# A 352-byte filler taken out of the constants, and two sets of small tiles moved into them: large left-side tiles from offset 32 (and 224, 160) to offset 0 of a 256-byte step

## The chip, the cores and the metric

The kernel runs on one core of one Trainium2 chip. Times are device microseconds (us) of one launch. A core has five engines with queues of their own: PE (TensorE, matrix products), ACT (ScalarE), DVE (VectorE), POOL (GpSimd) and SP (SyncE, which here issues every DMA). PE's product takes two operands from SBUF: one is loaded beforehand as weights (the profile has these loads as a row of their own, PEld), the other streams through (the moving operand). Results land in PSUM.

SBUF has 128 partitions; a tile takes the same bytes in each of them. "Offset" below always means a tile's first byte within the partition, and mostly what is left of it after division by 256.

## The reference, cut to what matters

One transformer block, batch 1, 1024 tokens, width 1024, all in float32:

```
mod = silu(c) @ w_ada + b_ada                       # six vectors: shift, scale, gate, twice
h   = rmsnorm(x, g) * (1 + sc1) + sh1
proj = h @ w_in                                     # attention q k v, delta q k v z, two gates
y_attn  = dilated attention, 8 heads, three branches merged by their log-sums
y_delta = gated delta rule, 8 heads, chunks of 64   # a recurrence over the chunks
x = x + g1 * (concat(y_attn, y_delta) @ w_out)
h = rmsnorm(x, g_ffn) * (1 + sc2) + sh2
x = x + g2 * ((silu(h @ w_gate) * (h @ w_up)) @ w_down)
out = rmsnorm(x, final_g)
```

## The kernel before

**Precision.** Every large product is made of three products in the faster float32r format: each operand is split into a high part (a rounded copy, made by ACT) and a low part (the rest, a subtraction on DVE or POOL), and high x high, high x low and low x high are added up in PSUM. So a weight block arrives by DMA in a raw tile `wr`, becomes `wh` and `wl`, and is used.

**Order of the work.** First the projections with the modulation (to about 135 us of the span). Then the delta rule's chunks, into whose gaps PE's projections for attention are filled by a table of due times (to 460 us); attention with the same filling (to 690 us); the output projection (to 749 us). Then the FFN. Its up products are arranged as a Strassen-like scheme with blocks called H11, H21, H22 and sums T1 to T4: for each of `NF` = 11 column blocks `f`, and for the gate and the up weights, there are seven blocks of 12 matmuls (`up_mm`, lines 1615 to 1625: four k, three products each): H11 and H21 in `up_first`, then T2, T1, T3, H22, T4 in `up_rest`. `up_mm` takes the weights (`wh`, `wl`) as PE's weights and the activations (`bh`, `bl`, halves of the H and T blocks) as the moving operand. The three first column blocks have their H11 and H21 parts done early (`AHEADF`, line 1756); the very first of these (f = 0, gate) has its weights in tiles of their own, `eh` and `el` (`slab_early`, line 1540). From 1172 us on come the down products (`down_mm`, line 1818, seven runs X, Y, X, Y2 (named Z in the profile), X, Z, X, with a tail W whose operands were prepared early, line 1839), and the last norm.

**How tiles are placed.** Pools on the left side of SBUF are stacked from the bottom, those on the right side from the top. The constants' pool `cp` is the lowest on the left; everything else on the left stands on it, so the size of the constants shifts all of it. By the program's list of placed tiles each tile's bytes are rounded up to 32. Offsets of the large tiles in the program before:

| pool, side | holds | first byte modulo 256 |
|---|---|---|
| `cp`, left | constants: `ident` and `onesr` (128), `S`, `beta` and others after the filler (32), `cc` (32) | mixed |
| `pr`, `pd`, left | inputs, delta rule | 32 |
| `pa` up to `sc`, left | attention: `va`, `KL`, `ng`, `X`; of `QS` and `KS` two buffers of three | 32 |
| `pa` after `sc`, left | `et`, `xo`, the third buffer of `QS` and `KS` | 224 |
| `pf`, `po`, `pe`, `px`, `po2`, left | FFN: H11 and H21, `eh`, `el`, sums, raw weights `wr2` | 32 |
| `pz` up to `rn`, left | down stage: gains, sums, `y` | 32 |
| `pz` after `rn`, left | `xr`, `sq3`, the early `wh` and `wl` of the tail W | 160 |
| `hh`, `hl`, `yh`, `yl`, `wp`, `wq`, `pt`, right | activations of the projections, all other `wr`, `wh`, `wl`, and H22, T1 to T4 | 0 |

The pool of the left side's FFN starts at byte 9504 = 37 x 256 + 32. On the right a filler of 224 bytes (line 98) is the first tile; it is not touched.

**Names that the change and the prediction touch.** `const([P, 88], "end")` (line 125) is the filler: 88 x 4 = 352 bytes. `sc` (line 1322, in `att_score`) holds, for one head and one block of 128 queries, the running minimum, the sum and its reciprocal; six buffers of 16 bytes rounded to 32, 192 bytes. `rn` (line 1864) holds the sums of squares of the last norm, 128 bytes.

Of the kernel before, what the change touches and what calls it, by code (L numbers as in the profile page):

```python
# [10 lines left out]
F32 = mybir.dt.float32  # L11
# [7 lines left out]
P = 128  # L19
# [63 lines left out]
def build(tc, I, out):  # L83
# [4 lines left out]
    def pool(name, side="left", bufs=1, space=None):  # L88
        st = ExitStack()
        kw = {} if space is None else {"space": space}  # L90
        p = st.enter_context(
            tc.tile_pool(name=name, bufs=bufs, side=side, reuse_waits="tile", **kw)
        )
        return p, st
# [4 lines left out]
    cp = op(tc.tile_pool(name="cp", bufs=1))  # L99
    dr = op(tc.tile_pool(name="dr", bufs=1, space=DRAM))  # L100

    def const(shape, name, dt=F32):
        return cp.tile(shape, dt, name=name, tag=name)
# [18 lines left out]
    mhalf = const([P, 4], "mhalf")  # L122
    nc.vector.memset(mhalf, -0.5)

    const([P, 88], "end")

    def small(name, shape, src):
        t = const(shape, name)
# [446 lines left out]
    @contextmanager  # L575
    def turn(name):

        with tc.issue_after(last[0].ins) if ahead(FILL.get(name, 0)) else ExitStack():
            yield
# [680 lines left out]
    pa, sa = pool("pa")  # L1260
    turns = [0]

    def scores(name):
        turns[0] += 1
        return abank(name) if turns[0] % 3 == 0 else sbank(name)
# [49 lines left out]
    def att_score(hp, qb, e):  # L1315

        h = 2 * hp + e
        nk = (qb + 1) * P
        qs = slice(qb * P, qb * P + P)
        QS, KS, KL, ng = loaded[hp][1][e]  # L1320
        X = pa.tile([P, T], F32, name=f"X{h}_{qb}", tag="X", bufs=XB)
        sc = pa.tile([P, 4], F32, name=f"sc{h}_{qb}", tag="sc", bufs=6)
        m = None
        for c0 in range(0, nk, HALF):
            c1 = min(nk, c0 + HALF)
            ps = scores(f"S{h}_{qb}_{c0}")
            with turn(f"S{h}_{qb}_{c0}"):
                nc.tensor.matmul(ps[:, 0 : c1 - c0], QS[:, qs], KS[:, c0:c1], start=True, stop=False)
                nc.tensor.matmul(ps[:, 0 : c1 - c0], QS[:, qs], KL[:, c0:c1], start=False, stop=True)  # L1329
            i = c0 // HALF  # L1330
            u = P * (7 - qb)
            nc.vector.tensor_tensor_reduce(  # L1332
                out=X[:, c0:c1], in0=ps[:, 0 : c1 - c0], in1=ng[:, u + c0 : u + c1], scale=1.0,
                scalar=(3e38 if m is None else m), op0=ALU.add, op1=ALU.min, accum_out=sc[:, i : i + 1],
            )
            m = sc[:, i : i + 1]
        nc.scalar.activation(X[:, 0:nk], X[:, 0:nk], AF.Exp, scale=-1.0, bias=m, accum_out=sc[:, 2:3])  # L1337
        nc.vector.reciprocal(sc[:, 3:4], sc[:, 2:3])  # L1338
        nc.gpsimd.tensor_scalar(  # L1339
            out=X[:, 0:nk], in0=X[:, 0:nk], scalar1=sc[:, 3:4], scalar2=0.0, op0=ALU.mult, op1=ALU.add  # L1340
        )
        return X
# [46 lines left out]
    def attend(switch):  # L1389
        units = [(hp, qb) for hp in range(4) for qb in range(TB)]  # L1390
        xs, ets = {}, {}
        for i in range(len(units) + AV):
            if i >= AV and units[i - AV] == (EARLY, 3):
                switch()
            if i < len(units):
                hp, qb = units[i]
                if hp not in loaded:
                    until(lambda: hp in done)
                    loaded[hp] = att_load(hp)
                if i < EARLY * TB + 3 + AV:  # L1400
                    ahead((FRONT - used[0]) / (EARLY * TB + 3 + AV - i))
                if qb >= 2 and hp < 3 and hp + 1 in done and hp + 1 not in loaded:
                    loaded[hp + 1] = att_load(hp + 1)
                xs[i] = [att_score(hp, qb, e) for e in range(2)]
            if AT <= i < len(units) + AT:
                hp, qb = units[i - AT]
                ets[i - AT] = [att_turn(hp, qb, e, xs[i - AT][e]) for e in range(2)]
                del xs[i - AT]
            if i >= AV and units[i - AV][1] % 2:
                hp, qb = units[i - AV]  # L1410
                att_value(hp, qb, [ets.pop(i - AV - 1), ets.pop(i - AV)])
# [385 lines left out]
    pz, sz = pool("pz")  # L1797
# [58 lines left out]
    def sums(name):  # L1856
        return [pz.tile([P, HALF], F32, name=f"{name}_{b}", tag=f"{name}{b}") for b in range(4)]
# [3 lines left out]

    p1, u2, r5 = sums("p1"), sums("u2"), sums("r5")
    y = {(l, s): sums(f"y{l}{s}") for l in range(2) for s in range(2)}
    rn = pz.tile([P, 8, 4], F32, name="rn", tag="rn")

    def x_in(l, s, b):
        x = pz.tile([P, HALF], F32, name=f"xr{l}{s}{b}", tag="xr", bufs=4)
# [160 lines left out]
```

## Time and profile before

| what | value |
|---|---|
| three runs | 1401.86, 1402.77 and 1393.12 us; median 1401.86 |
| the profiled execution's span, first to last instruction | 1389.5 us |
| the profiled execution's own time | about 1402.9 us: its trace's time axis begins 11.0 us before the first instruction, and its clock records end 2.3 us after the last one |
| instructions | 24383 |
| PE busy | 97% of the span, 8984 matmul records |
| DVE, ACT, POOL busy | 63%, 48%, 19% |
| DMA | 244.08 MB by SP's queue, 54.4% of 16 engines' span |
| granted clock of PE | 1.0 except in three stretches at 0.5: 10.2 us from 135.8 us of the span, 3.4 us from 794.5 us, and the last 6.8 us |

How to read it: a busy PE is not PE at its peak, since a matmul's record lasts longer than the time until the next one starts. In the chain of work that ended last, a row such as "PE wua L1622 x12" gives the time from the start of the first of 12 matmuls to the start of what follows, so it divides by 12 into the time from start to start. In a name like `wua<-H11h,wh_wu` the first name is what is written, the second the moving operand, the third the weights. Rows that group by line give minimum, median and maximum of the durations in ns.

### The profile page before, as it was taken

The page shows a single profiled execution, that of the slowest core. Times are in us where ns is not written, and L with a number is a line of the kernel's source. Part 1 is how long each engine was busy: PE and PEld are TensorE (multiplying, and loading weights), DVE is VectorE, ACT ScalarE, POOL GpSimd, SP SyncE. Part 2 cuts the span into 40 slices and gives each one's busy share as a digit, 9 for nine tenths or more (in the row PEclk, how much of TensorE's full clock was granted, in tenths as well). Part 3 has the DMA queues.
Part 4 walks back from the last instruction along what each step waited for, and adds up shares of the span by engine and source line. Part 5 has one row for each costly group of instructions (what it writes and reads, how often), then busy time and mean ns, then how long its engine had stood idle before and what let it go on. Part 6 is the DMA issues. An engine that isn't in the chain of part 4 may idle for free.

```text
span 1389.5 us, 24383 instructions
## 1 busy us (share of the span) xinstructions
PE 1343.3 (97%) x8984; PEld 1106.9 (80%) x8984; DVE 875.5 (63%) x1678; ACT 660.1 (48%) x1285; POOL 266.8 (19%) x250
## 2 busy tenths in 40 slices
PE   8998999999999999899999999999999999999998
PEld 4777887888889877678777788888888888888876
DVE  3687583657846242766258977666675776474497
ACT  4497514347233454775168533333333333444455
POOL 2345303324213433543261000000000000000000
PEclk9999899999999999999999999999999999999999
DMA  8666574476362546522675346444453665765585
GB/s 311 228 194 168 160 213 156 138 235 156 124 165 80 172 134 182 153 91 70 217 230 174 124 143 211 140 156 168 152 174 124 213 209 186 255 222 193 191 270 192
DMA packets 169871, 245.64 MB, mean 177 GB/s; under 512 B 32566, under 2 KB 73831, under 8 KB 169752
## 3 DMA queue, kind: packets, MB, share of 16 engines
q1 hardware_dynamic: 169752, 244.08, 54.4%
q8 instruction: 71, 1.16, 0.3%
q14 instruction: 48, 0.39, 0.1%
HBM read 181.27 MB, written 67.48 MB: 179 GB/s over the span
## 4 chain that ended last, share of the span: by engine, by line
PE 71%; DVE 14%; DMA 5%; ACT 4%; issue 3%; POOL 2%; SPq 0%; POOLq 0%; DVEq 0%; ACTq 0%
PE wua L1622 9%; PE wga L1622 8%; PE X L1822 6%; PE wuc L1622 4%; PE wgc L1622 4%; PE g_a L590 4%; PE wo L590 3%; PE Z L1822 3%; PE y L1373 2%; PE wub L1622 2%; PE wgb L1622 2%; PE Y L1822 2%; DVE tm L899 2%; PE g_va L616 2%; PE f L251 2%
## 5 line engine op out<-in xcount | busy, mean ns | idle before, releaser
L1612 DVE TENSOR_TENSOR wl_db<-wr_db,wh_db 128x512 fp32r<-128x512 f32 x77 | 52.8, 689 | 66.4 <-ACT wh_db L1611 66.4
L1611 ACT CAST wh_db<-wr_db 128x512 fp32r<-128x512 f32 x77 | 47.6, 621 | 86.3 <-PE X L1822 37.8
L1332 DVE CUSTOM_DVE_ANT_0 X<-S,ng 128x512 f32<-128x512 f32 (+3 forms) x64 | 36.6, 587 | 62.7 <-PE S L1329 54.7
L1339 POOL TENSOR_SCALAR X<-X,sc 128x128 f32<-128x128 f32 (+7 forms) x64 | 48.9, 767 | 90.4 <-DVE sc L1338 77.5
L1822 PE MATMUL X<-wl_db,wh_da 128*128 128x512 f32 x160 | 62.4, 390 | 0.3 <-DVE wl_db L1612 0.3
L1337 ACT ACTIVATE X<-X,sc 128x128 f32<-128x128 f32 (+7 forms) x64 | 49.4, 773 | 27.8 <-DVE sc L1332 26.3
L1822 PE MATMUL X<-wh_db,wl_da 128*128 128x512 f32 x160 | 62.3, 389 | 0.0
L1822 PE MATMUL X<-wh_db,wh_da 128*128 128x512 f32 x160 | 62.2, 389 | 0.0
L1612 DVE TENSOR_TENSOR wl_da<-wr_da,wh_da 128x512 fp32r<-128x512 f32 x77 | 52.8, 686 | 4.0 <-ACT wh_da L1611 4.0
L1611 ACT CAST wh_da<-wr_da 128x512 fp32r<-128x512 f32 x77 | 47.5, 617 | 14.2 <-DMA wr_da<-ao_d 7.8
L590 PE MATMUL wo<-yh,wh_wo 128*128 128x512 f32 x128 | 51.9, 406 | 0.0
L590 PE MATMUL g_a<-hh,wh_a 128*128 128x512 f32 x128 | 51.4, 401 | 0.0
L590 PE MATMUL wo<-yh,wl_wo 128*128 128x512 f32 x128 | 51.2, 400 | 0.0
L590 PE MATMUL wo<-yl,wh_wo 128*128 128x512 f32 x128 | 50.5, 395 | 0.5 <-DVE yl L1440 0.5
L590 PE MATMUL g_a<-hl,wh_a 128*128 128x512 f32 x128 | 50.7, 396 | 0.0
L590 PE MATMUL g_a<-hh,wl_a 128*128 128x512 f32 x128 | 50.4, 394 | 0.0
L1352 PE MATMUL tr<-ident,X 128*128 128x128 f32 x288 | 44.1, 277 | 4.7 <-ACT et L1357 2.3
L1611 ACT CAST wh_wg_s<-wg_s 128x512 fp32r<-128x512 f32 x33 | 20.5, 622 | 58.6 <-PE wuc L1622 24.8
L1352 PEld LDWEIGHTS tr<-ident,X 128*128 128x128 f32 x288 | 32.6, 140 | 15.9 <-POOL X L1339 7.2
L1611 ACT CAST wh_wu_s<-wu_s 128x512 fp32r<-128x512 f32 x33 | 20.4, 622 | 45.0 <-PE wga L1622 17.2
L1611 ACT CAST wh_wg<-wr_wg 128x512 fp32r<-128x512 f32 x31 | 19.3, 621 | 46.8 <-PE wua L1622 19.2
L231 POOL TENSOR_TENSOR wl_wo<-wr_wo,wh_wo 128x512 fp32r<-128x512 f32 x24 | 31.9, 1333 | 47.3 <-ACT wh_wo L230 43.1
(554 smaller groups left out, 4345.1 us busy)
## 6 DMA issues: line engine op xcount, KB each, us to landing
wm<-in_wada SPq DMA_DIRECT2D x44, 512.0 KB, 6.7
wr_da<-ao_d SPq DMA_DIRECT2D x77, 256.0 KB, 3.0
wr_wu<-in_wu SPq DMA_DIRECT2D x50, 256.0 KB, 2.8
wr_wg<-in_wg SPq DMA_DIRECT2D x48, 256.0 KB, 3.0
ao_d<-a SPq DMA_DIRECT2D x44, 256.0 KB, 2.5
wr_wd<-in_wdn SPq DMA_DIRECT2D x44, 256.0 KB, 3.0
wr_db<-wt_d SPq DMA_DIRECT2D x44, 256.0 KB, 3.0
ao_d<-as SPq DMA_DIRECT2D x33, 256.0 KB, 2.1
```

Of the source, the lines that this page charges most:

```text
L231: (eng or nc.gpsimd).tensor_tensor(out=lo[:, :n], in0=raw[:, :n], in1=hi[:, :n].bitcast(F32), op=ALU.subtract)
L251: nc.tensor.matmul(first[bank], a[:, w0], b[k][:, cs], start=(k == 0 and n_ == 0), stop=(k == KT - 1 and n_ == 2))
L590: last[0] = nc.tensor.matmul(ps, a[:, w0], b[k0 + k4][:, cs], start=(i == 0), stop=(i == n - 1))
L616: last[0] = nc.tensor.matmul(ps[:, :n], a[k][:, ts_], b[:, w0], start=(i == 0), stop=(i == 23))
L1332: nc.vector.tensor_tensor_reduce(out=X[:, c0:c1], in0=ps[:, 0 : c1 - c0], in1=ng[:, u + c0 : u + c1], scale=1.0, scalar=(3e38 if m is None ...
L1337: nc.scalar.activation(X[:, 0:nk], X[:, 0:nk], AF.Exp, scale=-1.0, bias=m, accum_out=sc[:, 2:3])
L1339: nc.gpsimd.tensor_scalar(out=X[:, 0:nk], in0=X[:, 0:nk], scalar1=sc[:, 3:4], scalar2=0.0, op0=ALU.mult, op1=ALU.add)
L1352: nc.tensor.transpose(ps[:, (kb - c0) * P : (kb - c0 + 1) * P], X[:, kb * P : kb * P + P], ident)
L1611: nc.scalar.copy(hi, src)
L1612: (eng or nc.vector).tensor_tensor(out=lo, in0=src, in1=hi.bitcast(F32), op=ALU.subtract)
L1622: nc.tensor.matmul(ps, a[:, w0], b, start=(first and k == 0 and n_ == 0), stop=(k == 3 and n_ == 2), skip_group_check=True,)
L1822: nc.tensor.matmul(bank[b], a[:, ts_], w, start=(first and n_ == 0), stop=(last and n_ == 2), skip_group_check=True,)
```

## The change

The filler in the constants goes, `sc` is allocated from the constants' pool and no longer from attention's, and `rn` becomes a constant instead of a tile of the last pool. No instruction is added, removed or reordered by the text of the change; only places in SBUF change.

```
@@ -122,7 +122,6 @@
     mhalf = const([P, 4], "mhalf")
     nc.vector.memset(mhalf, -0.5)
 
-    const([P, 88], "end")
 
     def small(name, shape, src):
         t = const(shape, name)
@@ -1319,7 +1318,7 @@
         qs = slice(qb * P, qb * P + P)
         QS, KS, KL, ng = loaded[hp][1][e]
         X = pa.tile([P, T], F32, name=f"X{h}_{qb}", tag="X", bufs=XB)
-        sc = pa.tile([P, 4], F32, name=f"sc{h}_{qb}", tag="sc", bufs=6)
+        sc = cp.tile([P, 4], F32, name=f"sc{h}_{qb}", tag="sc", bufs=6)
         m = None
         for c0 in range(0, nk, HALF):
             c1 = min(nk, c0 + HALF)
@@ -1861,7 +1860,7 @@
 
     p1, u2, r5 = sums("p1"), sums("u2"), sums("r5")
     y = {(l, s): sums(f"y{l}{s}") for l in range(2) for s in range(2)}
-    rn = pz.tile([P, 8, 4], F32, name="rn", tag="rn")
+    rn = const([P, 8, 4], "rn")
 
     def x_in(l, s, b):
         x = pz.tile([P, HALF], F32, name=f"xr{l}{s}{b}", tag="xr", bufs=4)
```

In bytes: the constants lose 352 and gain 192 and 128, together 32 fewer, so what stands on them starts at 9504 - 32 = 9472 = 37 x 256. With `sc` gone from attention's pool, what stood after it moves from 224 to 0, and with `rn` gone from the last pool, what stood after that moves from 160 to 0. The right side stays where it is. Constants between the old filler and the end of the pool move by 352 bytes, from offset 32 to 192 (`S`, for one).

More of the change, by code (lines that the diff above doesn't have):

```diff
@@ L123, in build @@
     nc.vector.memset(mhalf, -0.5)
-    const([P, 88], "end")
     def small(name, shape, src):
@@ L1321, in att_score @@
         X = pa.tile([P, T], F32, name=f"X{h}_{qb}", tag="X", bufs=XB)
-        sc = pa.tile([P, 4], F32, name=f"sc{h}_{qb}", tag="sc", bufs=6)
+        sc = cp.tile([P, 4], F32, name=f"sc{h}_{qb}", tag="sc", bufs=6)
         m = None
@@ L1863, in build @@
     y = {(l, s): sums(f"y{l}{s}") for l in range(2) for s in range(2)}
-    rn = pz.tile([P, 8, 4], F32, name="rn", tag="rn")
+    rn = const([P, 8, 4], "rn")
     def x_in(l, s, b):
```

## The prediction, made before the changed kernel was run

> **What bounds the kernel now.** I read the page first: the span and the chain of work that ended last, by engine and by line.
>
> ```profile
> span 1389.5 us, 24383 instructions
> ...
> PE 71%; DVE 14%; DMA 5%; ACT 4%; issue 3%; POOL 2%; SPq 0%; POOLq 0%; DVEq 0%; ACTq 0%
> PE wua L1622 9%; PE wga L1622 8%; PE X L1822 6%; PE wuc L1622 4%; PE wgc L1622 4%; PE g_a L590 4%; PE wo L590 3%; PE Z L1822 3%; PE y L1373 2%; PE wub L1622 2%; PE wgb L1622 2%; PE Y L1822 2%; DVE tm L899 2%; PE g_va L616 2%; PE f L251 2%
> ```
>
> PE carries 71% of the chain, and the FFN's up blocks (`wua` to `wgb`) are its largest part. The change moves tiles and nothing else, so the question is what an offset costs, and whether PE pays it. Stretches of the span come next; after the borders stand PE, its weight loads, DVE, ACT and POOL (busy, count), then granted clock, DMA share, GB/s.
>
> ```profile
> 135.70:146.00 10.30, 10.30 (x78) 10.30 (x77) 6.76 (x12) 10.30 (x33) 2.88 (x3) 0.50 0.66 154
> 794.50:798.00 3.50, 3.50 (x10) 2.69 (x10) 3.50 (x7) 2.15 (x4) 0.00 (x0) 0.51 0.50 166
> 810.00:1172.00 362.00, 362.00 (x1584) 297.02 (x1583) 245.32 (x383) 132.05 (x226) 0.00 (x0) 1.00 0.50 169
> 1172.00:1375.00 203.00, 201.97 (x885) 165.35 (x885) 134.25 (x226) 103.48 (x194) 0.00 (x0) 1.00 0.68 230
> ```
>
> From 810 to 1172 us, the up products, PE never rests: what a matmul takes there is time of the kernel. DVE is busy 245 of 362 us, so it can feed a PE that is a per cent faster. The two first rows are stretches at half clock; they come back among the rivals.
>
> **The key row.** The chain in order of time shows one pass of the up products, block by block: start, us, what, and how many.
>
> ```profile
> 959.20 2.80 PE wua L1622 x12
> 962.01 2.80 PE wub L1622 x12
> 964.81 2.76 PE wua L1622 x12
> 967.56 2.72 PE wuc L1622 x12
> 970.28 2.72 PE wua L1622 x12
> 973.00 2.72 PE wuc L1622 x12
> 975.72 2.72 PE wua L1622 x12
> ```
>
> All are blocks of 12 matmuls of one shape. In order they are H11, H21, T2, T1, T3, H22, T4. The last four take 2.72 us, 226.7 ns each. H11 and H21 take 2.80 us: 233.4 ns. T2, which follows them, takes 2.76 us. H11 and H21 are the two blocks that stand on the left, at offset 32, with weights from the right, at offset 0; T1 to T4 and H22 stand on the right. That may be the offset, or it may be that these two blocks come first. Durations by operand (minimum/median/maximum, ns):
>
> ```profile
> L1622 PE MATMUL wua<-H11h,wh_wu x44: 393/396/479, 749.3 to 1153.5; 128*128 128x512 f32 x44
> ...
> L1622 PE MATMUL wga<-T4h,wh_wg x44: 389/389/389, 788.2 to 1150.8; 128*128 128x512 f32 x44
> ```
>
> ```profile
> L1822 PE MATMUL W<-wh_db,wh_da x16: 387/389/390, 1371.9 to 1382.1; 128*128 128x512 f32 x16
> ```
>
> W's operands stand on the left too, at offset 160, but both of them: no penalty. So offset from a multiple of 256 isn't the trouble by itself; a difference between the two operands' offsets may be. The pass f = 0 of the gate tests this. There H11 at 32 meets weights `eh` and `el` that are also at 32. PE in order of time, two pairs of rows, each pair seven starts apart:
>
> ```profile
> 741.24 0.39 PE L1622 MATMUL wga<-H11h,el 128*128 128x512 f32 x1
> ...
> 742.83 0.39 PE L1622 MATMUL wgb<-H21h,eh 128*128 128x512 f32 x1
> ```
>
> ```profile
> 940.50 0.40 PE L1622 MATMUL wga<-H11h,wh_wg 128*128 128x512 f32 x1
> ...
> 942.14 0.39 PE L1622 MATMUL wga<-H11l,wh_wg 128*128 128x512 f32 x1
> ```
>
> With `eh` 1.59 / 7 = 227 ns, with `wh_wg` 1.64 / 7 = 234 ns: the same activations from the same place, and only the weights' offset differs. I take it that a matmul of 512 columns in this format takes 6.7 ns more while weights are loaded from another offset, modulo 256, than it streams from.
>
> **The change part by part.**
>
> *H11 and H21 from offset 32 to 0.* Both operands are then at 0. Of 22 passes (11 column blocks, gate and up) one has `eh` and is free of the penalty already: 21 x 2 blocks x (2.80 - 2.72) us = 3.4 us.
>
> *T2 behind them.* Its 2.76 us are, I think, a settling after the slower rhythm: its offsets agree, and it ends at the pace of T1. In the passes f = 3 to 10 it follows H21 directly (f < 3 had H11 and H21 done early): 16 x 0.04 us = 0.6 us. Both terms lie on the path, as PE is busy 362.00 of 362 us there. Together 4.0 us.
>
> *Mixed stages, 135 to 690 us.* Products with operands at 0 alternate with short matmuls on left tiles at 32 or 224. A price falls where one follows the other; by my count in PE's order, with the placements, some 155 matmuls of the fast format have their successor's weights at 32 now. At 6.7 ns that is 1.0 us, at the least nothing; a few scores of `KL` (32) with `QS` at 224 lie inside that. I take 0.5 us. The weights' path into transposes stays unequal (`ident` at 128).
>
> *Constants that lose agreement.* `S` goes to 192 while `kd` and `qd` go to 0; today both are at 32. These are 112 matmuls of 128 columns in plain float32. What unequal offsets cost in that format is seen in transposes against `ident`, at 128 against 32:
>
> ```profile
> L1352 PE MATMUL tr<-ident,X x288: 270/272/332, 466.6 to 651.3; 128*128 128x128 f32 x144
> ```
>
> ```profile
> L998 PE MATMUL st<-S,kd x56: 270/275/348, 253.4 to 445.1; 128*128 128x128 f32 x56
> ```
>
> Unequal 272 ns, equal 275: no price. Taken as 0; at most 112 x 6.7 ns = 0.8 us.
>
> *`sc` and `rn`.* The same instructions, buffers and engines, no new wait. A loss would need slower small operations, and those work on one column wherever they stand.
>
> ```profile
> L1338 DVE RECIPROCAL sc<-sc x64: 142/164/168, 459.9 to 648.7; 128x1 f32<-128x1 f32 x64
> ```
>
> Without `sc` and `rn` below them, attention's later tiles and the last pool's overlap no more of the older tiles than before (I went through the placements); so no transfer waits for more. Taken as 0 on both sides.
>
> *Vector engines.* Subtractions whose source is mostly a raw tile on the right at 0 (first row, some are on the left) and one on the left at 32 (second) take the same:
>
> ```profile
> L1612 DVE TENSOR_TENSOR wl_wu<-wr_wu,wh_wu x33: 679/684/693, 743.9 to 1157.9; 128x512 fp32r<-128x512 f32 x33
> L1612 DVE TENSOR_TENSOR wl_wg_s<-wg_s,wh_wg_s x33: 681/685/695, 767.1 to 1135.7; 128x512 fp32r<-128x512 f32 x33
> ```
>
> Nothing there, and DVE isn't the bound.
>
> *DMAs.* All of 256 KB; columns are KB each and median us to landing.
>
> ```profile
> wr_da<-ao_d SPq DMA_DIRECT2D x77, 256.0 KB, 3.0
> ...
> wr_wd<-in_wdn SPq DMA_DIRECT2D x44, 256.0 KB, 3.0
> ...
> wr_db<-in_wdn SPq DMA_DIRECT2D x33, 256.0 KB, 3.4
> ...
> wr_wo<-in_wo SPq DMA_DIRECT2D x24, 256.0 KB, 2.6
> ...
> xo<-in_xT SPq DMA_DIRECT2D x16, 256.0 KB, 3.4
> ```
>
> `wr_wd` lands on the left at 32, `wr_da` and `wr_db` on the right at 0: the left is no slower, and from the same tensor (`in_wdn`) it is faster. `xo` (left, 224) against `wr_wo` (right, 0) is the one pair that speaks for a price, 0.8 us of 3.4, but its source is read in half rows. DMA has 5% of the chain, 69.5 us; at 0.8 / 3.4 that would be 16 us at most. Two pairs of three show none, so I take 0. [...]
>
> **The sum.** 4.0 + 0.5 = 4.5 us. The profiled execution's own time is about 1402.9 us (span 1389.5, and 13.3 around it), close to the median, so the median can stand for it: 1401.9 - 4.5 = **1397.4 us**, 0.3% less. A measurement of this kernel can tell about 1% from no change.
>
> **The rivals.**
>
> *Nothing changes: 1401.9 us.* The 6.7 ns could belong to the blocks' place in the order, or the tiles could end up elsewhere than the byte sums say. For it: H11 and H21 always come first. Against: the pass with `eh` comes first too and runs at 227 ns. [...] Chance 0.15.
>
> *The clock: 1390.6 us.* The stretches at half clock (10.3 us at 0.50 and 3.5 us at 0.51) cost half their length, 5.1 + 1.7 us. Slightly other timing may do without them: 1397.4 - 6.8 = 1390.6. For it: the fastest of three runs is 8.7 us below the median. Against: two of three runs are not. Chance 0.15.
>
> *DMAs gain as well: 1389.2 us.* If `xo` against `wr_wo` is the true price and half of the chain's DMA time has it, 16 / 2 = 8.2 us go besides. Against: the other pairs, and that PE never rests in the up stage, so nothing there waits for a transfer. Chance 0.10.
>
> *Equal offsets collide: slower, 1413.9 us.* Today DVE and ACT work on the left at 32 while PE reads at 0 on the right; after the change all are at 0. If PE then meets them as it meets its own weight loads now, the 1584 + 885 matmuls from 810 to 1375 us pay 6.7 ns each: 16.5 us. It decides once more than 4.5 us / 6.7 ns = 670 of them pay. Against: T4's 389/389/389 is steady while DVE reads and writes `wr`, `wh` and `wl` at 0. Chance 0.05.
>
> **How the numbers follow.** The forecast has the remaining 0.55; its own range is 1394 to 1400. The range of 1387.5 to 1402.5 takes in the clock case, "nothing" and most of the DMA case; left out are the collision, the far end of the DMA bound, and both rivals with a gain at once. Faster by over 1% means below 1387.8: parts of the clock and DMA cases, 0.09. Slower by over 1% means above 1415.9: 0.02. Within 1%: 0.89.
>
> **What would show it.** In the chain after, H11 and H21 at 2.72 us for 12, T2 at 2.72, the stretch of one pass 0.20 us shorter; `wua<-H11h,wh_wu` at a median of 389. W stays at 389, `st<-S,kd` near 275, DMA landings as they are. Wrong would be: H blocks still at 2.80 (the cause is not the offset), T1 to T4 above 2.72 (collision), or landings on the left shorter by over 0.3 us with a shorter first 135 us (the DMA case).

## The result, and the profile after

| | median of 17 runs | lowest to highest |
|---|---|---|
| before | 1393.4 us | 1388.4 to 1409.3 |
| after | 1385.8 us | 1382.1 to 1394.5 |

The ratio of after to before is 0.9942, with a 95% interval of 0.9923 to 0.9961: 8.1 us gained (5.4 to 10.7), where 4.5 us were forecast. It is inside the 1% of the prediction, but the interval is clear of 1. The three times that the prediction started from had a median of 1401.9 us; 17 have 1393.4. So the kernel came out below the forecast range, at more gain than forecast and from a lower start. Executions more than 1.5% above the fastest of their kernel are left out of every ratio and count below.

The profiled execution after has a span of 1383.3 us, 6.2 less. From the page, with the chain by engine:

```profile
span 1383.3 us, 24383 instructions
...
PE 71%; DVE 14%; DMA 5%; ACT 4%; issue 3%; POOL 2%; SPq 0%; POOLq 0%; DVEq 0%; ACTq 0%
```

The bound is the same. The chain in order of time, the same stretch as in the prediction (line numbers are one lower, since a line is gone):

```profile
955.40 2.72 PE wua L1621 x12
958.12 2.72 PE wub L1621 x12
960.84 2.72 PE wua L1621 x12
963.56 2.72 PE wuc L1621 x12
966.28 2.72 PE wua L1621 x12
969.00 2.72 PE wuc L1621 x12
971.72 2.72 PE wua L1621 x12
```

H11, H21 and T2 took 2.80, 2.80 and 2.76 us and now take 2.72 like the others. The same in two rows of durations:

```profile
L1621 PE MATMUL wua<-H11h,wh_wu x44: 389/389/476, 748.9 to 1147.7; 128*128 128x512 f32 x44
...
L1821 PE MATMUL W<-wh_db,wh_da x16: 389/389/389, 1365.7 to 1375.9; 128*128 128x512 f32 x16
```

H11's median fell from 396 to 389 ns, and W, equal offsets before and after, stayed. How long the up stage is, the first product of the down stage shows (first row before, second after):

```profile
L1822 PE MATMUL X<-wh_db,wh_da x160: 387/389/396, 1170.7 to 1371.2; 128*128 128x512 f32 x160
```

```profile
L1821 PE MATMUL X<-wh_db,wh_da x160: 388/389/389, 1164.7 to 1365.1; 128*128 128x512 f32 x160
```

From the first `wua<-H11h` to the first X it is 1170.7 - 749.3 = 421.4 us before, 1164.7 - 748.9 = 415.8 after: 5.6 less. Windows after, the columns as in the prediction:

```profile
135.70:146.00 10.30, 10.30 (x87) 10.30 (x87) 7.02 (x11) 10.30 (x32) 2.88 (x3) 0.54 0.63 163
794.50:798.00 3.50, 3.50 (x17) 2.88 (x16) 3.50 (x7) 2.32 (x5) 0.00 (x0) 1.00 0.79 241
810.00:1172.00 362.00, 362.00 (x1599) 299.77 (x1598) 246.87 (x386) 133.01 (x228) 0.00 (x0) 1.00 0.51 171
```

The half-clock stretch at 794.5 us is gone (17 matmuls in place of 10, so 7 x 0.227 = 1.6 us); the one at 135.7 is still there. So 5.6 - 1.6 = 4.0 us of the up stage are the blocks, as forecast. In these two executions nothing else is left over: 4.0 + 1.6, 0.4 up to the first `wua`, and 0.2 after the first X make the 6.2. The runs, however, gained 8.1 by the ratio.

Transfers, KB each and median us to landing, after:

```profile
wr_da<-ao_d SPq DMA_DIRECT2D x77, 256.0 KB, 2.9
...
wr_wd<-in_wdn SPq DMA_DIRECT2D x44, 256.0 KB, 3.0
...
wr_db<-in_wdn SPq DMA_DIRECT2D x33, 256.0 KB, 3.4
...
xo<-in_xT SPq DMA_DIRECT2D x16, 256.0 KB, 3.8
```

`xo` went from offset 224 to 0 and lands no sooner (3.4 before). One transfer that the prediction didn't look at does: the second 512 KB into `tn`, where the delta rule's chunk solve begins. Before, then after; the first row is the product that reads it, the second the issue, the third who waited:

```profile
L931 PE MATMUL lv<-tn,dt x64: 191/191/212, 387.0 to 388.0; 32*32 32x32 f32 x64
...
L908 SPq DMA_DIRECT2D tn<-tn_d x1: 370/370/370, 381.3 to 381.3; - x1
...
  PE lv L931: 0.6, 1
```

```profile
L930 PE MATMUL lv<-tn,dt x96: 191/191/212, 386.3 to 395.7; 32*32 32x32 f32 x96
...
L907 SPq DMA_DIRECT2D tn<-tn_d x1: 371/371/371, 381.4 to 381.4; - x1
```

From issue to use that is 5.6 us before and 4.9 after, without rounding, and PE's wait of 0.6 us is gone from the list. The chain that ended last goes through this landing; first before, then after:

```profile
381.35 5.58 DMA tn<-tn_d
```

```profile
381.40 4.78 DMA tn<-tn_d
```

### The profile page after: what moved, and what is told of

It reads as the page before. It is cut to its first block, busy times and chain, and to the rows that moved or that the text cites. A ratio compares the mean times of both kernels' runs of the same rounds, so it can differ in the third digit from the quotient of the medians.

```text
span 1383.3 us, 24383 instructions
## 1 busy us (share of the span) xinstructions
PE 1336.5 (97%) x8984; PEld 1105.9 (80%) x8984; DVE 875.4 (63%) x1678; ACT 659.7 (48%) x1285; POOL 268.4 (19%) x250
## 4 chain that ended last, share of the span: by engine, by line
PE 71%; DVE 14%; DMA 5%; ACT 4%; issue 3%; POOL 2%; SPq 0%; POOLq 0%; DVEq 0%; ACTq 0%
PE wua L1621 9%; PE wga L1621 8%; PE X L1821 6%; PE wgc L1621 4%; PE wuc L1621 4%; PE g_a L589 4%; PE wo L589 3%; PE Z L1821 3%; PE Y L1821 2%; PE wub L1621 2%; PE wgb L1621 2%; PE y L1372 2%; PE g_va L615 2%; DVE tm L898 2%; PE f L250 2%
```

## The experiments

**Theory A** is the prediction's: a matmul of the fast format with 512 columns pays some 6.7 ns while moving operand and weights differ in offset modulo 256. The other theories are in the expectations. "Low" below counts executions with a mean granted clock of 0.990 or less; the expectations' own counts were made on the way, some with 0.991 as the border, and differ by a few. The kernels ran in five groups (on the chips numbered 1, 4, 10, 6 and again 1), each group beside the kernel before, and the ratios are to that.

| kernel | H11, H21 against their weights | `tn` at | ratio to before (95%) | H11, H21, T2 us | `tn` issue to use us | low |
|---|---|---|---|---|---|---|
| before | 32 / 0 | 32 | 1 | 2.80, 2.80, 2.76 | 5.6 | 61 of 144 |
| changed | 0 / 0 | 0 | 0.9942, 0.9934, 0.9942, 0.9951 | 2.72, 2.72, 2.72 | 4.7 to 4.9 | 6 of 47 |
| left32 | 32 / 0 | 32 | 1.0007 (0.9983 to 1.0031) | 2.80, 2.80, 2.76 | 5.6 | 9 of 12 |
| right32 | 0 / 32 | 0 | 0.9974 (0.9952 to 0.9995) | 2.80, 2.80, 2.75 | 4.6 | 0 of 12 |
| both32 | 32 / 32 | 32 | 0.9945 (0.9912 to 0.9977) | 2.72, 2.72, 2.72 | 5.6 | 2 of 8 |
| ffn_only | 0 / 0 | 32 | 0.9990 (0.9967 to 1.0012) | 2.72, 2.72, 2.72 | 5.7 | 6 of 12 |
| ffn32 | 32 / 0 | 0 | 0.9970 (0.9943 to 0.9997) | 2.80, 2.80, 2.76 | 4.8 | 1 of 12 |
| moves_undone | 0 / 0 | 0 | 0.9962 (0.9937 to 0.9987) | 2.72, 2.72, 2.72 | 5.0 | 2 of 12 |
| sc_back | 0 / 0 | 0 | 0.9952 (0.9932 to 0.9972) | 2.72, 2.72, 2.72 | 4.8 | 0 of 12 |
| delta32 | 0 / 0 | 32 | 0.9964 (0.9936 to 0.9991) | 2.72, 2.72, 2.72 | 5.6 | 3 of 11 |
| delta0 | 32 / 0 | 0 | 0.9968 (0.9943 to 0.9994) | 2.80, 2.80, 2.76 | 4.8 | 3 of 12 |
| left64 | 64 / 0 | 64 | 0.9992 (0.9965 to 1.0020) | 2.76, 2.75, 2.77 | 5.6 | 6 of 11 |
| left128 | 128 / 0 | 128 | 0.9971 (0.9949 to 0.9994) | 2.79, 2.80, 2.73 | 4.8 | 2 of 12 |
| pr32 | 0 / 0 | 32 | 0.9980 (0.9947 to 1.0013) | 2.72, 2.72, 2.72 | 5.6 | 4 of 12 |
| pr0 | 32 / 0 | 0 | 0.9976 (0.9950 to 1.0003) | 2.80, 2.80, 2.76 | 5.0 | 2 of 12 |
| pr0_ffn | 0 / 0 | 0 | 0.9955 (0.9932 to 0.9977) | 2.72, 2.72, 2.72 | 4.7 | 0 of 12 |

### Is it the difference of the offsets?

**left32**, the changed kernel with 32 bytes put back where the filler was:

```
     nc.vector.memset(mhalf, -0.5)
+    const([P, 8], "end")
```

> The changed kernel with 32 bytes of filler put back: left tiles at 32 again, but sc and rn still among the constants. Theory A (a matmul of the fast format pays about 6.7 ns while its moving operand and the weights loaded beside it differ modulo 256): H11 and H21 at 2.80 us for 12 again and T2 at 2.76, so the up stage is 4.0 us longer than in the changed kernel; median 4 us above it, ratio to the kernel before 0.997 to 1.000. Theory B (the gain is that of sc and rn, or of the later tiles of attention and of the down stage): the time stays at that of the changed kernel, ratio 0.994. Theory C (the part of the gain beyond 4 us is the clock's half-speed stretches, which come and go with the timing): the up stage as A says, and the rest moves with the granted clock of each run, whatever the offsets.

1.0007: the gain is gone, though `sc` and `rn` are where the changed kernel has them. Theory B falls. But 10 us were lost against the changed kernel beside it (1.0007 - 0.9934 = 0.73%), not 4, and 9 of 12 executions are low (median 1400.3 us; the other three 1390.7): as theory C has it, the rest goes with the granted clock. Theory C's "whatever the offsets" is what the second group of experiments tries.

**right32**, the right side at 32 and the left at 0:

```
-    ends.tile([P, 56], F32, name="end", tag="end")
+    ends.tile([P, 48], F32, name="end", tag="end")
```

> The changed kernel with the right side's filler cut from 224 to 192 bytes: left at 0, everything on the right at 32. Theory A (difference of the two operands' offsets): H11 and H21 at 2.80 us for 12, T2 at 2.76, and T1, T3, H22, T4 at 2.72, as in the kernel before: ratio 0.997 to 1.000. Rival D (each operand that does not begin on a multiple of 256 costs): T1 to T4 and H22 at 2.80 as well, 22 x 5 x 0.08 = 9 us more in the up stage and 885 x 6.7 ns = 6 us more in the down stage than in the changed kernel, 10 us slower than the kernel before: ratio 1.008.

The chain of right32, one pass:

```profile
960.04 2.80 PE wua L1621 x12
962.84 2.80 PE wub L1621 x12
965.64 2.75 PE wua L1621 x12
968.39 2.72 PE wuc L1621 x12
```

H11 and H21, now the aligned ones, are slow; T1, on the right at 32 with its weights at 32, is not. Rival D (every operand off a multiple of 256 costs) falls here already.

**both32**, both edits at once:

> Left and right both at 32: nothing large begins on a multiple of 256. Theory A (difference of the two operands' offsets): every block of the up stage at 2.72 us for 12 and the time that of the changed kernel within 0.2%, ratio 0.994. Rival D (distance from a multiple of 256): all seven blocks at 2.80, the up and down stages together 15 us longer than in the changed kernel plus the H blocks' 4: ratio 1.008 or more.

```profile
957.75 2.72 PE wga L1622 x12
960.47 2.72 PE wgb L1622 x12
963.19 2.72 PE wga L1622 x12
```

A pass of the gate, its first blocks, H11 first: all at 2.72 us with not one large tile on a multiple of 256. Theory A stands. The time is the changed kernel's (0.9945), though the interval of eight executions reaches to 0.998.

**offsets** leaves the block out and runs rows of 36 matmuls with chosen offsets; its output is other numbers:

```
+    def run(name, pairs, n=36, cols=512, mt=None, wt=None):
+        ps = pg.tile([P, HALF], F32, name=name, tag="ps", bufs=4)
+        m_, w_ = mt or mv, wt or (wa, wb)
+        for i in range(n):
+            m, w = pairs[i % len(pairs)]
+            m, w = OFF[m] // 4, OFF[w] // 4
+            nc.tensor.matmul(ps[:, 0:cols], w_[i % 2][:, w : w + P], m_[:, m : m + cols], start=(i == 0), stop=(i == n - 1))
```

> No block of the transformer: rows of 36 matmuls (128 x 512, fast format, weights from two tiles in turn) on operands whose offsets are set one by one; the output is filled with other numbers. Theory A (the moving operand's offset against that of the weights loaded beside it, modulo 256): 226.7 ns from start to start wherever the two are equal (0/0, 32/32, 64/64, 128/128, and 256/0), 233.4 ns wherever they differ. Rival D (each distance from a multiple of 256 costs): 32/32 and 64/64 slow too. [...] Of the two rows with offsets in turn, theory A expects the one whose weights equal their own moving operand but not the next weights to be slow, and the one whose next weights equal the moving operand to be fast. Plain float32 with 32/0: no price above 1%.

The chain in order of time; after m stands the moving operand's offset, after w that of the weights: z 0, h 32, s 64, o 128, f 256.

```profile
41.07 8.16 PE mz_wz L114 x36
49.23 8.40 PE mh_wz L114 x36
57.64 8.25 PE ms_wz L114 x36
...
74.30 8.40 PE mo_wz L114 x36
...
107.92 8.39 PE mz_wh L114 x36
116.32 8.19 PE mh_wh L114 x36
...
325.03 8.16 PE mf_wz L114 x36
...
341.35 8.36 PE own L114 x36
349.71 8.30 PE nxt L114 x36
358.01 4.31 PE half_mz_wz L114 x36
362.32 4.25 PE half_mh_wz L114 x36
...
374.55 13.79 PE plain_mz_wz L114 x32
388.34 13.73 PE plain_mh_wz L114 x32
```

Divide by 36: 226.7 ns at 0/0, 227.5 at 32/32 (the first few settle), 226.7 at 256/0; 233.1 to 233.3 at 32/0, 128/0 and 0/32. Rival D falls, and a step of 128 is not free either. The price is 6.4 to 6.6 ns here; the chain of before gave 6.7. A moving operand 64 bytes beyond the weights pays less (229.2), so theory A's one price for every difference is not right in this case: 2.5 ns, not 6.4 to 6.6. With 256 columns (118 ns with the difference, 120 without) and in plain float32 (429 and 431) there is no price. One thing came out otherwise: with offsets in turn, `own` and `nxt` both lie between fast and slow (232 and 231 ns), so the runs don't say whether a matmul minds its own weights or the next ones.

**left64** and **left128** put 64 and 128 bytes in the filler's place (`const([P, 16], "end")`, `const([P, 32], "end")`).

> The changed kernel with 64 bytes of filler put into the constants: the whole left at 64, the right at 0. From the rows of single offsets (moving operand 64 beyond the weights: 228.8 ns from start to start, 32 beyond: 233.3, none: 226.7): H11 and H21 at 2.745 us for 12, so 21 x 2 x 0.025 = 1.1 us and up to 0.6 for T2 more than in the changed kernel's up stage. Rival (any difference has one price): H11 and H21 at 2.80, 4.0 us more. Theory F in the form that any offset but 0 brings long stretches: half of the executions at or below 0.991; in the form that only 32 does: 2 of 12 at most.

> The changed kernel with 128 bytes of filler put into the constants: the whole left at 128, the right at 0. By the rows of single offsets the price of a difference of 128 is that of 32 (233.3 against 226.7 ns): H11 and H21 at 2.80 us for 12 and the up stage 4.0 us longer than in the changed kernel. Theory F in the form that any offset of the delta rule's tiles but 0 brings the long stretches: about half of the executions at or below 0.990, ratio 0.998 to 1.001. In the form that 128 is even enough: at most 2 of 12, ratio 0.996 to 0.998.

H11, H21 and T2 of left64, then of left128:

```profile
960.52 2.76 PE wua L1622 x12
963.29 2.75 PE wub L1622 x12
966.03 2.77 PE wua L1622 x12
```

```profile
956.07 2.79 PE wua L1622 x12
958.86 2.80 PE wub L1622 x12
961.66 2.73 PE wua L1622 x12
```

At 64 the pass is 0.12 us over 3 x 2.72, so 21 x 0.12 = 2.5 us: less than the 4.2 of a difference of 32 (21 x 0.20), more than the 1.1 to 1.7 expected. The largest part is T2: 2.77 us, 0.05 over 2.72, with H11 and H21 0.04 and 0.03 over. At 128 it is 0.16, or 3.4 us, near the 4.0 expected. From the first `wua<-H11h` to the first X the stage is 2.2 and 3.3 us longer than in the changed kernel. The low executions are the other finding: 6 of 11 at 64, 2 of 12 at 128. If the offset brings them, its step is 128 bytes; the matmul pays at a difference of 128 (233.3 ns) and not at one of 256 (226.7).

### Where are the other 4 us?

**ffn_only** pads the FFN's pool alone in the kernel before, **ffn32** the same pool in the changed one:

```
     pf, sf = pool("pf")
+    pf.tile([P, 56], F32, name="pad", tag="pad")      # ffn32: [P, 8]
```

> The kernel before with 224 bytes of filler ahead of the FFN's left tiles only: H11 and H21 at 0, the stages before (delta rule, attention) and the tail W where they were. Theory A for the up stage: H11 and H21 at 2.72 us, 4.0 us less than before, ratio 0.997. Theory F (the rest of the gain comes from the delta rule's and attention's tiles, by fewer or shorter stretches at half clock there): the long stretch at half clock near 390 us and executions of a granted clock of 0.986 to 0.990 stay as frequent as in the kernel before (about 16 of 28), and no more than the 4.0 us are gained. Rival G (the whole gain is the FFN's): ratio 0.994.

> The changed kernel with 32 bytes of filler ahead of the FFN's left tiles only: H11 and H21 at 32, the stages before as in the changed kernel at 0. Theory A: H11 and H21 at 2.80 us, 4.0 us more than the changed kernel. Theory F (fewer stretches at half clock with the delta rule's and attention's tiles at 0): executions of a clock at or below 0.990 are rare (2 of 35 so far with the left at 0), so the median is 4 us above that of the changed kernel, some 1390, ratio 0.997. Rival G (the whole gain is the FFN's): ratio 1.000 and long stretches as often as before.

Each part alone gives some 0.1 to 0.3%. Rival G (all of it in the FFN) falls: it asked for 0.994 of ffn_only, whose interval ends at 0.9967, and for 1.000 of ffn32, which is faster than before (if barely, to 0.9997) with its H blocks at 2.80. And the low executions go with what stands ahead of the FFN: 6 of 12 against 1 of 12.

**moves_undone** leaves `sc` and `rn` where they were and only cuts the filler to 80 floats; **sc_back** moves only `sc` back:

```
-    const([P, 88], "end")
+    const([P, 80], "end")
```

> The kernel before with its filler cut from 352 to 320 bytes, sc in attention's pool and rn in the last pool as before: left base at 0, attention's tiles after sc at 192, the last pool's after rn at 128, S at 0. Theory A: H11 and H21 at 2.72 us; the up stage as in the changed kernel. Theory B (sc and rn, or the later tiles of attention and the down stage, carry part of the gain): 1 us or more above the changed kernel. Without theory B: the time of the changed kernel within 0.15%, ratio 0.993 to 0.995. Theory F (delta rule's tiles at 0 keep the long stretches at half clock away): few executions at a clock of 0.990 or less.

> The changed kernel with sc back in attention's pool and 192 bytes of filler in the constants instead: left base at 0, rn still a constant, attention's et, xo and third buffers of QS and KS at 192. Theory B for sc (executions without long stretches had a median near 1389.6 us with sc and rn in their old places and the base at 0, against 1385.4 in the changed kernel): near 1389 us, ratio 0.996. Rival I (those 4 us are chance or rn's): 1385 to 1386.5 us, ratio 0.993 to 0.994.

0.9962 and 0.9952. The changed kernel ran beside sc_back and had 0.9942 (medians 1389.0 and 1388.8 us): what looked like 4 us for `sc` was a difference between groups. moves_undone had no changed kernel beside it, and its 0.9962 lies above the 0.993 to 0.995 expected without theory B, though its interval takes them in. So `rn` is left to pr0_ffn below, which has both tiles in their old places.

**delta32** (the delta rule at 32 in the changed kernel) and **delta0** (the delta rule at 0, attention and the FFN at 32):

```
     pr, sr = pool("pr")
+    pr.tile([P, 8], F32, name="pad", tag="pad")       # delta32 only
...
     pa, sa = pool("pa")
+    pa.tile([P, 56], F32, name="pad2", tag="pad2")    # delta0: [P, 8], and [P, 8] in pf
```

> The changed kernel with 32 bytes of filler ahead of the delta rule's tiles and 224 ahead of attention's: the delta rule at 32 as in the kernel before (with two of three buffers of QS and KS), attention's other tiles and the FFN at 0 as in the changed one. Theory F, narrowed to the delta rule (long stretches at half clock come when its tiles stand at 32): about half of the executions at a granted clock of 0.991 or less (with the left at 32 before the FFN it was 47 of 92 so far, at 0 it was 5 of 59) and those some 8 us longer; up stage as in the changed kernel; ratio 0.996 to 0.998. Rival H (attention's tiles or chance): at most 2 of 12 such executions, ratio 0.993 to 0.995.

> The changed kernel with 32 bytes of filler ahead of attention's tiles and 32 ahead of the FFN's: only the delta rule (and two buffers of QS and KS) at 0, everything later on the left at 32. Theory F, narrowed to the delta rule (executions at a granted clock of 0.990 or less were 5 of 83 with its tiles at 0, 74 of 151 with them at 32 or 64): at most 2 of 12 such executions, H11 and H21 at 2.80 us for 12, ratio 0.996 to 0.998, as with only the FFN at 32. Rival (attention's tiles bring the long stretches, as two buffers at 32 beside the delta rule's left some doubt): 5 or more of 12.

3 of 11 and 3 of 12: taken alone these two don't separate anything. What did was laying all profiles beside each other, matmul by matmul in PE's order: from 340 to 412 us those with the delta rule at 32 or 64 fall 0.9 to 1.2 us behind the changed kernel, most of it at the first product that reads `tn`, and those at 0 or 128 no more than 0.2 (profiles with a half-clock stretch in that part set aside). The table's column for `tn` is what came of it. `tn` is written in pieces of 32 floats, 128 bytes: at 0 and 128 they end on multiples of 128, at 32 and 64 each of them crosses one, which for every second piece is a multiple of 256.

The traces hold the pieces one by one, 4096 in the second transfer. In the twelve profiles with `tn` at 0 or 128 none takes more than 13 ns, 12.9 on average; in the seven at 32 or 64, 1013 to 1265 of them take longer, up to 46 ns, 15.7 to 16.4 on average. As an estimate, 4096 pieces x 2.8 to 3.5 ns on 16 engines are 0.7 to 0.9 us, the whole of the delay. So it arises in the transfer itself. Whether it is the crossing that costs, and of 128 or of 256, these offsets don't tell.

**pr32** shifts, in the changed kernel, only the pool that holds `tn` (and `nt`, `tt`, `eb`, `xp` and two buffers of `QS` and `KS`); **pr0** takes only that pool to 0 in the kernel before; **pr0_ffn** does so and pads the FFN as ffn_only does:

```
     pr, sr = pool("pr")
+    pr.tile([P, 8], F32, name="pad_pr", tag="pad_pr")      # pr0: [P, 56]
     pd, sd = pool("pd")
+    pd.tile([P, 56], F32, name="pad_pd", tag="pad_pd")     # pr0: [P, 8]
...
     pa, sa = pool("pa")
+    pa.tile([P, 56], F32, name="pad_pa", tag="pad_pa")     # pr0: [P, 8]
```

> The changed kernel with only the first pool of the delta rule (tn, nt, tt, QS, KS) at 32, everything else on the left at 0. Theory J (the 512 KB transfer into tn, in pieces of 128 bytes, lands 0.8 us later at 32 or 64 than at 0 or 128, so the chunk solve and PE wait 0.8 us longer near 387 us, and that longer pause brings the long half-clock stretch): from the issue of tn's second transfer to the first product that reads it 5.6 us (4.8 in the changed kernel), executions at a granted clock of 0.990 or less in a third to a half of the cases, ratio 0.996 to 0.998, H11 and H21 at 2.72 us. Rival K (other tiles of the delta rule, read by PE or DVE, bring the stretches): 4.8 us or 5.6, but at most 1 of 12 such executions, ratio 0.993 to 0.995.

> The kernel before with only that first pool (tn, nt, tt, QS, KS) at 0 and the rest of the left at 32 as before. Theory J: tn 4.8 us from issue to use instead of 5.6, executions at a clock of 0.990 or less rare (10 of 107 so far with tn at 0 or 128, 74 of 164 at 32 or 64), the up stage as before: ratio 0.997 to 0.998. Rival K: 0.999 to 1.001 and such executions as frequent as in the kernel before.

> The kernel before with that first pool and the FFN's left tiles at 0, all else of the left (the rest of the delta rule, attention, tail W) at 32, 224 and 160 as before, sc and rn in their old places. Theory J with theory A: these two explain the whole change, so the time is the changed kernel's within 0.15% (ratio 0.993 to 0.996) though most of the left stands at 32. Rival: 2 us or more above the changed kernel, if attention's tiles, sc or rn carry a part.

In pr32 the transfer is late again, and PE waits for it:

```profile
L932 PE MATMUL lv<-tn,dt x64: 191/191/212, 388.6 to 389.6; 32*32 32x32 f32 x64
...
L909 SPq DMA_DIRECT2D tn<-tn_d x1: 371/371/371, 383.0 to 383.0; - x1
...
  PE lv L932: 0.7, 1
```

In pr0 it isn't (5.0 us), though PE still waits 0.5 us there. So the lateness belongs to this pool's offset; that is shown in all 19 profiles: the landing in the chain takes 5.5 to 5.7 us in the seven with `tn` at 32 or 64 and 4.6 to 5.0 in the twelve at 0 or 128. PE's own wait says less: 0.5 to 1.1 us in the seven, 0 to 0.6 in the twelve. pr0_ffn is the test of the whole: attention, the rest of the delta rule and W stand at 32, 224 and 160 as before, `sc` and `rn` are in their old places, and it runs like the changed kernel beside it (0.9955 and 0.9951). Theory B is out, and two places are the change, within the 0.2% that the intervals leave.

**after_again**, **after_third** and **after_fourth** are the changed kernel beside the others:

> The changed kernel once more, beside the others. All theories: ratio 0.992 to 0.996 to the kernel before. Theory C (half-speed stretches of the clock explain the part of the gain beyond 4 us): a second profile shows a stretch at half clock elsewhere or of other length than the first, and executions of a lower mean granted clock are the long ones; theory B (sc, rn or transfers): the stages before 690 us are shorter than in the kernel before by 3 us.

> The changed kernel a third time, beside the three others: a median of 1385 to 1386 us, ratio 0.992 to 0.995, at most 2 executions at a granted clock of 0.991 or less.

> The changed kernel beside the three others: 1385 to 1389 us, ratio 0.992 to 0.996, at most 1 or 2 executions at a clock of 0.990 or less.

The ratios are 0.9934, 0.9942 and 0.9951; the medians (1385.6, 1388.8 and 1387.7 us) move from group to group, so the third missed its expectation, and in the last group 4 of 12 were low, more than expected. The last was profiled in a low execution. Windows, with columns as before:

```profile
390.00:407.50 17.50, 17.50 (x222) 15.41 (x211) 6.25 (x14) 4.12 (x11) 2.21 (x3) 0.51 0.27 91
```

and left32's profile, low as well:

```profile
394.00:413.00 19.00, 18.31 (x238) 16.12 (x238) 7.20 (x16) 5.24 (x14) 2.21 (x3) 0.55 0.28 85
```

What the two low profiles share is 17.1 us at half clock within these windows, in the chunk solve, from some 3.3 us behind the start of the product that waited for `tn` (left32's has 10.2 us more from 258.6 us, and both32's profile 47.8 us from 2.0 us behind that product). It happens with `tn` early too, as in after_fourth, but less often: 16 of 143 executions of all kernels with `tn` at 0 or 128, 91 of 210 with it at 32 or 64. Side by side in the last group, pr0 and pr0_ffn had 2 of 24 where the kernel before had 13 of 34; but pr32 (4 of 12) did not differ from the changed kernel (4 of 12). And the length of PE's pause doesn't decide it: the wait for `tn` was 0.5 and 0.6 us in the two low profiles, and 1.1 us in ffn_only and delta32, which have no such stretch. That this pool's offset changes how often the stretch comes is what the counts show; that the late `tn` is what brings it, as theory J has it, is not shown.

## Why the prediction was right or wrong

**The key row and its price: right.** H11, H21 and T2 went to 2.72 us, 4.0 us of the up stage, and left32, right32, both32 and the rows of single offsets show the cause to be what was claimed, a difference of offsets. The rival that nothing changes falls: PE does lose 6.4 to 6.7 ns on 226.7 at a difference of 32. Only that the price is the same for every difference was too simple (64 bytes beyond the weights it is 2.5 ns in the rows of single offsets, 229.2 against 226.7).

**The base: wrong, and this alone put the time out of the range.** The step was "the profiled execution's own time is about 1402.9 us (span 1389.5, and 13.3 around it), close to the median, so the median can stand for it". In every execution listed since, the time is the span plus 1.95 to 2.29 us (1385.31 for 1383.3). The profiled execution before was therefore one of 1391.5 us, 10.4 below the median of three. From there the forecast's own 4.5 us lead to 1387.0. Two of the three times, 1401.9 and 1402.8, were low executions, to go by their length: of 144 runs of the kernel before, 61 are low with a median of 1399.5 us, and 83 are not, with a median of 1392.7 and none above 1397.8. That two of three fell on the low side was bad luck, but no rare one (at 61 in 144, as an estimate, in 39% of such triples). The profile and the median of three belonged to different kinds of execution, and 13.3 us of unexplained surroundings were the sign of it.

**"Two pairs of three show none, so I take 0" (DMAs): the step of the sum that failed.** Rows of 2048 bytes indeed show no price, and `xo` at 0 lands at 3.8 us, 3.4 at 224. But the pairs were all of 256 KB in long rows, and `tn`, 512 KB in pieces of 128 bytes, was not looked at; it is 0.8 us later at 32, and it lies on the path (the chain goes through its landing, before and after). At 64 it is as late as at 32 (5.6 us from issue to use), at 128 as early as at 0 (4.8). What in the transfer makes a piece take longer there is not shown.

**The clock rival: the right actor, the wrong stretch.** It let the stretches at 135.7 and 794.5 us vanish. The first is in every profile, 6.8 to 10.2 us long. What mattered is a long stretch near 390 us that the profile of before didn't hold, because its execution wasn't a low one. The changed kernel has 6 low executions in 47, the kernel before 61 in 144. Low ones are 1399.5 - 1392.7 = 6.8 us longer, so (0.42 - 0.13) x 6.8 = 2.0 us of the mean gain. PE's pauses don't tell the executions apart: in the ten us ahead of the stretches of left32 and after_fourth the two longest are 0.5 to 0.6 and 0.8 us, and the profile of before has such a pair, 0.6 and 0.8 us, without a stretch. Why it comes in one execution and not in the next is open.

**The sum, closed.** The five kernels with only the early `tn` (right32, ffn32, delta0, left128, pr0) have a mean ratio of 0.9972; the four with only H at its weights' offset (both32, ffn_only, delta32, pr32) 0.9970. Each single ratio is uncertain by some 0.25%, but together the parts make 0.28 + 0.30 = 0.58%, the whole of what was measured; that they meet this closely is luck, since both32 alone (0.9945, with the late `tn`) lies 0.25% below the mean of its group. In us that is 4.2 for the blocks, of which the trace shows 4.0, and 3.9 for `tn` and its pool: 0.8 of lateness, 2.0 of rarer low executions, and some 1 us that has no place.

**The rest.** `sc` and `rn` at 0: right. W unchanged and `st<-S,kd` free of price: right (its median is 275 ns before and after, and plain float32 showed no price in the rows of single offsets either). The 0.5 us for the mixed stages can't be told apart: apart from `tn`, one execution's stages before the FFN differ from the next one's by more. The collision: no block of the pass shown went above 2.72 us.

No kernel tried beats the changed one; pr0_ffn equals it.

## What to carry to other kernels

Compare the offsets of the two operands of a matmul, modulo 256, rather than each one's alignment: here a 3% price on 512-column blocks (2.80 against 2.72 us for 12) went away with both at 32 as well as with both at 0. When tiles move, look first at the transfers made of the smallest pieces, and at those whose landing something waits for, since rows of 2 KB said nothing about pieces of 128 bytes here (`xo` landed at 3.4 us at 224 and at 3.8 at 0, `tn` 0.8 us later at 32 than at 0). And before a forecast is set on a median of few runs, ask whether the profiled execution is of their kind: here its span plus 2 us and their median were 10 us apart, more than the change was worth.

## What of the hardware was not expected

- The matmul's price has a pattern: in the rows of single offsets it went with the moving operand's offset minus the weights'. Over its 36 starts a row runs at 226.7 to 227.5 ns for 0 and 226.7 for 256 either way, 229.2 for +64 at each of four pairs, 232.5 to 234.4 for other multiples of 32, and 227.2 for weights 16 bytes beyond the moving operand (but 231.4 the other way round).
- After a change from unequal to equal offsets some matmuls run at other times before they settle at 227 ns: in T2 of before, at 2.76 us, the first seven take 224 to 241 ns, and the rows 32/32, 64/64 and 128/128 took 8.19 us for 36 where 0/0 took 8.16.
- A transfer of 512 KB in pieces of 128 bytes landed 0.8 us later (5.6 against 4.8 us) with its tile at 32 or 64 than at 0 or 128: a quarter to three in ten of its pieces took over 13 ns, where otherwise none did.
- PE ran at half clock for 17.1 us while it counted as busy throughout (17.50 of 17.50 us in after_fourth), in a stage with many 32 x 32 matmuls, and behind pauses of no more than 0.8 us. Low executions are two in five with `tn`'s pool at 32 or 64 (91 of 210) and one in nine with it at 0 or 128 (16 of 143).
